# Five pads of 32 to 96 bytes that move activation tiles in SBUF, in a float32 two-block transformer on one core

## The chip, the cores and the metric

The kernel runs on one core of a Trainium2 chip (trn2). The metric is the device time of one execution in microseconds; the median of three runs of the kernel before is 1934.56 us (1934.15 to 1935.23). The other seven cores do nothing.

## The reference

One sequence of 256 tokens with 1024 features passes two blocks in float32. The first block is a mixer (retention in four heads, differential attention in four heads, both over the sequence and 256 context tokens) and a layer of 16384 single-neuron experts, of which eight retrieval heads choose 16 each per token. The second is a short convolution, attention to 256 memory tokens, a SwiGLU layer, causal attention in eight heads, memory attention and SwiGLU again. Cut to what carries the time:

```python
x = x + mod[:, 2] * (concat([ret_lat, diff_lat]) @ w_out)   # mixer
h2 = modulate(x, norm2_g, mod[:, 3], mod[:, 4])
u, vsel = expert_u[experts], expert_v[experts]              # 8 heads x 16 of 16384
act = gelu(einsum('thkd,td->thk', u, h2))
x = x + mod[:, 5] * einsum('thk,thkd->td', gate * act, vsel)
# second block: conv mixer, memory attention, SwiGLU, attention, memory attention, SwiGLU
```

## The kernel before

**Data.** Activations lie transposed in SBUF, 128 features on the partitions, eight chunks of features and 256 tokens on the free axis, so one chunk of one tile is 256 float32 values, 1024 bytes, on each partition. Weights stream through SBUF once, in tiles of 1024 values per partition (4096 bytes).

**The product.** A float32 product is three float32r passes. Each operand is split into a part that float32r holds (hi) and the rest (lo). `split_w` (L106 to L120) makes `whi` by a copy on ScalarE (L111) and `wlo` by a subtraction on VectorE or GpSimd (L115). `mm3` (L131) then issues, for eight chunks k, hi by hi, lo weight by hi and hi weight by lo, 24 matmuls into one PSUM bank (L137). Every matmul loads its own 128 by 128 stationary operand first (the rows on PEld). In `mm3` the weights are stationary and the activations are moved, 256 columns at a time:

```python
order = [(s, i) for s in range(3) for i in range(n)]
...
self.matmul = nc.tensor.matmul(out, a, b, start=..., stop=...)   # a stationary (weights), b moved
```

In `natural_steps` (L172) and in the expert product (L945) it is the other way round: the activations (`hh`, `hmh`, `acth`) are stationary and the weights are moved, 256 columns in the first, 512 in the second.

**The stages, in order of time.** Adaln parameters and the norm (to 92 us); mixer (to 306): gate, key, query and value products of `hh`, `hl`, attention, output product of `cath`, `catl` (L137), with tiles of the memory keys (`hmh`, `hml`) put in between; expert layer (306 to 1157): 16 query blocks and then 128 blocks of `peer_u`, 24 matmuls each, that move `h2h`, `h2l`. Beside them VectorE does the routing (top-k, L763 to L803), and after it, from `R1` = 16 pairs of blocks on, `group` (L867 to L885) builds the gates for four tokens at a time: GpSimd makes `ohA` (L861) and multiplies into `slots` (L882), VectorE and ScalarE make `ohB` (L862, L864), TensorE multiplies them (L876). 64 groups are spread over 96 blocks, so one group goes with 36 matmuls of `h2`. Then the expert product, 128 chunks of 12 matmuls (L945). The second block follows: convolution (1160 to 1277), memory attention, SwiGLU (`hh`, then `fh`, `fl`), attention (`hh`, `hqh`, `oh`), memory attention, SwiGLU, final norm.

**Where the tiles lie.** Pools are opened as a stack. A tile takes its size rounded up to 32 bytes, and a pool opens where the last open one ends. So a tile of 8 or 64 bytes early in a pool shifts all that opens later. The weight pool (`raw`, `whi`, `wlo`, L103, L109, L110) opens at byte 30432 and holds multiples of 4096: every weight tile starts at byte 224 of 512, which is byte 96 of 128. The starts of the others, counted in this way, on each partition, and those with the pads of the change counted in the same way:

| tiles | start before | of 512, before | of 512, with the pads |
|---|---|---|---|
| weights `whi`, `wlo` | 42720 and on | 224 | 224 |
| mixer `hh`, `hl` | 67296 | 224 | 256 |
| memory keys ahead, `hmh`, `hml` | 116480 | 256 | 288 |
| mixer `cath`, `catl` | 151936 | 384 | 416 |
| experts `slots`, `h2h`, `h2l`, `ohA`, `ohB`, `acth`, `actl` | 63200 and on | 224 | 256 |
| second memory, `memk1`, `memv1`, `hmh`, `hml` | 67296 | 224 | 256 |
| convolution `hh`, `hl`, `ch`, `cl` | 164704 | 352 | 0 |
| memory attention and SwiGLU `hh`, `fh`, `oh`; attention `hh` | 127744 and on | 256 | 384 |
| attention `hqh`, `hql`, `oh` | 164640 and on | 288 | 416 |

The chunks of these tiles and the columns of the weights go on in steps of 512 or 1024 bytes, so the place within 512 bytes holds for each matmul of a tile.

Of the kernel before, what the change touches and what calls it, by code (L numbers as in the profile page):

```python
"""A two-part transformer in one launch.

Activations lie transposed, features on the partitions and tokens on the free axis, and stay in
SBUF from the first norm to the last. Weights stream through SBUF once. A float32 product is
carried by three float32r passes: each operand is split into a part that float32r holds exactly
and the rest (hi + lo), and hi*hi + hi*lo + lo*hi are accumulated in PSUM.
"""
# [8 lines left out]
F32 = mybir.dt.float32  # L16
# [6 lines left out]
PSUM = bass.MemoryType.PSUM  # L23
DRAM = bass.MemoryType.DRAM

P = 128
T = 256
# [42 lines left out]
class Build:  # L70
# [14 lines left out]

    def banks(self, ctx, name):
        """The banks of one phase: mm and, by the phase, sc and aux or pairs of banks."""
        self.ps = ctx.enter_context(self.tc.tile_pool(name="psum" + name, bufs=2, space=PSUM))
# [5 lines left out]
    def after(self, ins, other):  # L94
        """Issue order only: no wait."""
# [22 lines left out]
    def weight(self, src, lo=None):  # L118
        """hi and lo of a weight tile. lo: the engine of the subtraction."""
# [7 lines left out]
    def mm3(self, out, pairs, first=True, last=True, late=False):  # L127
        """out += sum of w^T x over (w_hi, w_lo, x_hi, x_lo), three passes each; late: pair by pair."""
# [10 lines left out]
    def fill(self, n):  # L139
        """n tiles of the work that depends on nothing near."""  # L140
        for _ in range(n):
            next(self.filler, None)
# [6 lines left out]
    def block(self, out, src, x, cols=slice(None), lo=None, late=False, w=None):  # L149
        """out[128 n, tokens] = W block^T x, the weights stationary."""  # L150
# [8 lines left out]
    def natural_steps(self, tag, srcs, toks, done, lo=None):  # L159
        """x^T W with the tokens stationary, 256 columns of W (two tiles of srcs) at a time; two  # L160
        token blocks share a bank. done(n, i, bank) takes the columns n of the token blocks 2i, 2i + 1."""
# [26 lines left out]
    def rstd(self, pool, sums, n, tag, shape=(P, T), bufs=1, a=None, y=None, tables=False, behind=None):  # L188
        """(sums / n + eps) ** -0.5, a Newton step after the tables."""
# [19 lines left out]
    def track(self, x, m, tags=("acc", "accsq"), bufs=2):  # L209
        """Adds the squares of chunk m of eight to the sum over chunks; the last stays apart."""  # L210
# [10 lines left out]
    def tracked_norm(self, pool, tag, bank="aux", urgent=False, last=None, **kw):  # L221
        """rstd over the features of the chunks tracked, the same on every partition; last: behind the matmuls
        so far."""
# [17 lines left out]
    def modulated(self, pool, tags, x, r, A, Bv, h, cols):  # L241
        """h[:, :, cols] = x * r * A + B, split."""
# [8 lines left out]
    def gained(self, pool, x, gi, name="h"):  # L251
        """x * g (no rstd yet), split."""
# [46 lines left out]
    def mod_group(self, pool, g):  # L299
        """512 of the adaln parameters, for c and for c_ctx: the rows of o are hi c, hi c_ctx, lo c, lo c_ctx."""  # L300
# [31 lines left out]
    def mod_rest(self, pool, groups):  # L332
        """gate1, shift2, scale2, gate2 for c, a piece at a time."""
        nc, io = self.nc, self.io
        late = []
# [34 lines left out]
    def rope_out(self, pool, q, out, cos, sin):  # L370
        """out = q * cos + rot(q) * sin for q [128, 256] in SBUF; sin has the signs of rot, which swaps the halves
        of every 32 partitions."""
# [7 lines left out]
    def decay(self, pool, M):  # L380
        """M [j, t] for j in x and in ctx, by head: [128, 4 heads, 4 key chunks, 256]. The logarithms of the
        rates are not positive, so the smaller of the two exponents is the one for the sign of the distance."""
# [1235 lines left out]
```

## Time and profile before

| | |
|---|---|
| median of the runs (lowest, highest) | 1934.56 us (1934.15, 1935.23) |
| profiled execution, span | 1934.6 us |
| mean granted TensorE clock | 0.976 of full speed |
| HBM read | 329.59 MB, 172 GB/s over the span |

The profiled execution's own time is its span, from the first instruction to the last. A row of the timeline gives the start, the length from there, the engine, line and operation, the tiles as output <- moved operand, stationary operand, and the number of instructions merged. [...]

### The profile page before, as it was taken

What the parts mean: (1) busy time and instruction counts of PE and PEld (TensorE: products, weight loads), DVE (VectorE), ACT (ScalarE), POOL (GpSimd) and SP (SyncE); (2) the same over time, 40 slices, a digit from 0 to 9 for tenths busy, and PEclk for the clock granted to TensorE, in tenths of its full rate; (3) what the DMA queues carried; (4) which work ended last, traced back from release to release, by engine and by line L of the source; (5) the groups of instructions that cost most, each with busy time, mean ns of one, the idle gap of its engine ahead of it and who ended that gap; (6) DMA issues with size and microseconds to landing.
All of it is one profiled execution on the core that took longest, in us unless ns stands there. A gap on an engine that the chain in (4) does not pass through costs nothing.

```text
span 1934.6 us, 34858 instructions
## 1 busy us (share of the span) xinstructions
PE 1838.1 (95%) x13232; PEld 1717.9 (89%) x13232; DVE 1465.7 (76%) x2646; ACT 1043.2 (54%) x1775; POOL 587.3 (30%) x508
## 2 busy tenths in 40 slices
PE   5899999994999999999999998999999999999997
PEld 4697788994999999878888878999999998999997
DVE  8988966999988999865555568676765578677664
ACT  5645534542777777554554455455554544555543
POOL 2511113782888999400000004222000213110001
PEclk8999999997999999999999998999999999999999
DMA  7672434452444444655555555553555553435553
GB/s 261 218 250 93 137 131 154 170 179 76 167 161 164 164 153 160 225 195 194 196 195 191 192 184 177 185 185 132 195 187 187 187 179 130 158 127 186 187 191 124
DMA packets 99768, 335.15 MB, mean 173 GB/s; under 512 B 12400, under 2 KB 13456, under 8 KB 99216
## 3 DMA queue, kind: packets, MB, share of 16 engines
q1 hardware_dynamic: 98160, 330.68, 49.5%
q8 instruction: 105, 1.72, 0.4%
q10 hardware_dynamic: 1440, 2.23, 0.3%
q14 instruction: 63, 0.52, 0.1%
HBM read 329.59 MB, written 3.28 MB: 172 GB/s over the span
## 4 chain that ended last, share of the span: by engine, by line
PE 69%; DVE 16%; POOL 9%; DMA 2%; issue 2%; ACT 2%; SPq 0%; DVEq 0%; ACTq 0%; POOLq 0%
PE mm L137 40%; PE pair L945 17%; POOL ohA L861 5%; PE mm L172 4%; POOL slots L882 3%; PE fill L137 2%; DVE wlo L115 2%; PE fill L172 2%; DVE slots L798 1%; DVE slots L795 1%; PE pair L876 1%; PE sc L137 1%; DVE slots L773 1%; PE aux L137 1%; DVE mlo L115 1%
## 5 line engine op out<-in xcount | busy, mean ns | idle before, releaser
L111 ACT CAST whi<-raw 128x1024 fp32r<-128x1024 f32 x564 | 591.4, 1050 | 517.5 <-PE mm L137 261.0
L115 DVE TENSOR_TENSOR wlo<-raw,whi 128x1024 fp32r<-128x1024 f32 x490 | 623.9, 1276 | 297.7 <-PE pair L945 129.3
L115 POOL TENSOR_TENSOR wlo<-raw,whi 128x1024 fp32r<-128x1024 f32 x74 | 186.5, 2522 | 199.1 <-PE mm L137 109.0
L861 POOL TENSOR_SCALAR ohA<-iota,selT 128x128 fp32r<-128x128 f32 x256 | 191.1, 762 | 53.2 <-ACT selT L829 32.5
L219 POOL TENSOR_TENSOR acc<-acc,accsq 128x256 f32<-128x256 f32 x42 | 37.9, 903 | 497.9 <-ACT accsq L217 497.9
L137 PE MATMUL mm<-hh,whi 128*128 128x256 f32 (+1 forms) x1184 | 180.0, 289 | 6.2 <-DVE ct L1243 4.4
L137 PE MATMUL mm<-hl,whi 128*128 128x256 f32 (+1 forms) x1184 | 177.1, 287 | 1.0 <-DVE hl L262 0.9
L137 PE MATMUL mm<-hh,wlo 128*128 128x256 f32 (+1 forms) x1184 | 175.7, 286 | 0.6 <-DVE wlo L115 0.6
L137 PE MATMUL mm<-h2h,whi 128*128 128x256 f32 x1152 | 167.6, 288 | 4.1 <-ACT h2h L247 4.0
L137 PEld LDWEIGHTS mm<-hh,whi 128*128 128x128 f32 x1184 | 156.5, 190 | 11.1 <-issue 6.8
L137 PE MATMUL mm<-h2h,wlo 128*128 128x256 f32 x1152 | 163.4, 284 | 0.0
L137 PE MATMUL mm<-h2l,whi 128*128 128x256 f32 x1152 | 162.4, 284 | 0.0
L945 PE MATMUL pair<-whi,acth 128*128 128x512 f32 x512 | 158.4, 391 | 1.0 <-ACT acth L937 1.0
L137 PEld LDWEIGHTS mm<-hh,wlo 128*128 128x128 f32 x1184 | 155.0, 190 | 4.4 <-issue 1.5
L945 PE MATMUL pair<-whi,actl 128*128 128x512 f32 x512 | 158.2, 390 | 0.3 <-DVE actl L938 0.3
L137 PEld LDWEIGHTS mm<-hl,whi 128*128 128x128 f32 x1184 | 155.2, 190 | 3.4 <-DVE hl L262 1.6
L945 PE MATMUL pair<-wlo,acth 128*128 128x512 f32 x512 | 157.8, 389 | 0.0
L137 PEld LDWEIGHTS mm<-h2h,whi 128*128 128x128 f32 x1152 | 151.9, 195 | 5.0 <-ACT h2h L247 4.8
L137 PEld LDWEIGHTS mm<-h2h,wlo 128*128 128x128 f32 x1152 | 150.1, 193 | 0.0
L137 PEld LDWEIGHTS mm<-h2l,whi 128*128 128x128 f32 x1152 | 149.3, 193 | 0.0
L1083 POOL TENSOR_TENSOR memk0l<-kvt,memk0h 128x512 fp32r<-128x512 f32 x4 | 6.4, 1611 | 378.9 <-ACT memk0h L1082 378.9
L945 PEld LDWEIGHTS pair<-whi,acth 128*128 128x128 f32 x512 | 95.5, 188 | 22.1 <-ACT acth L937 2.6
(416 smaller groups left out, 3454.2 us busy)
## 6 DMA issues: line engine op xcount, KB each, us to landing
raw<-peer_u SPq DMA_DIRECT2D x128, 512.0 KB, 3.5
raw<-peer_v SPq DMA_DIRECT2D x128, 512.0 KB, 3.4
raw<-ffn_gu SPq DMA_DIRECT2D x88, 512.0 KB, 3.6
raw<-ffn_dn SPq DMA_DIRECT2D x44, 512.0 KB, 3.5
raw<-w_mod SPq DMA_DIRECT2D x64, 256.0 KB, 4.1
raw<-conv_wi SPq DMA_DIRECT2D x24, 512.0 KB, 3.5
raw<-mem_wk SPq DMA_DIRECT2D x16, 512.0 KB, 4.5
mraw<-w_mod SPq DMA_DIRECT2D x16, 512.0 KB, 6.4
```

The costliest lines, as they stand in the source:

```text
L111: self.hi_copy = nc.scalar.copy(hi, raw)
L115: (nc.vector if plan == "v" else nc.gpsimd).tensor_sub(lo, raw, hi)
L137: self.matmul = nc.tensor.matmul(out, a, b, start=first and j == 0, stop=last and j == 3 * n - 1)
L172: self.matmul = nc.tensor.matmul(outs[i // 2][:, i % 2], a[:, k, :], b[:, w], start=k == 0 and s == 0 and i % 2 == 0, stop=k == 7 and s == ...
L219: self.adder.tensor_add(self.acc, self.acc, self.last)
L773: nc.vector.tensor_tensor(cand, vv[:, :, 0, :, None].to_broadcast([P, 2, 16, 16]), vv[:, :, 1, None, :].to_broadcast([P, 2, 16, 16]), op=O ...
L795: nc.vector.tensor_tensor(one, pb[:, :, :, None].to_broadcast([P, 2, 16, 16]), self.iota[:, None, None, 0:16].to_broadcast([P, 2, 16, 16]) ...
L798: nc.vector.tensor_tensor(one, one, ii[:, :, side, None, :].to_broadcast([P, 2, 16, 16]), op=OP.mult)
L861: nc.gpsimd.tensor_scalar(A[:, i], self.iota, selT[:, 1, t:t + 1], None, op0=OP.is_equal)
L876: nc.tensor.matmul(o[:, 2 * j + i], A[:, i], Bt[:, i], start=True, stop=True)
L882: getattr(nc, GMUL).tensor_mul(sl, lo[:, :, :done], sl)
L945: nc.tensor.matmul(acc[th][:, dh], x[:, tsl], wt[:, dh * 512:dh * 512 + 512], start=c == 0 and s == 0, stop=c == NCH - 1 and s == 2)
```

## The change

A new helper puts a small tile into a pool, with a memset on VectorE that nothing reads. It is called in five places: first in the mixer's pool (32 bytes), first in the pool of `slots` (32), after `conv_w` in the convolution's pool (32), first in the pool `sums` of the second block (32) and first in the pool `side` (96 bytes). The weight pool opens ahead of all five. Comments are blanked besides.

```diff
+    def shift(self, pool, n=8):
+
+        self.nc.vector.memset(pool.tile([P, n], F32, name="shift"), 0.0)
+
...
             pool = self.pool(ctx, "mix")
+            self.shift(pool)
             rg = pool.tile([P, 4, T], F32, name="rg")
...
             big = self.pool(ctx, "slots")
+            self.shift(big)
             pool = self.pool(ctx, "peer")
...
             cw = self.load(pool, "conv_w", [P, KC, 3])
+            self.shift(pool)
             h = self.gained(pool, self.x, G_MIX)
...
                 b.sums = b.pool(c2, "sums")
+                b.shift(b.sums)
                 kvp = b.pool(c2, "kv")
                 side = b.pool(c2, "side")
+                b.shift(side, 24)
                 kv1, b.filler = b.mem_fill(kvp, side, 1)
```

## Rows read from the trace of the kernel before

**Rows 1.** The page, part 1: busy time of each engine, share of the span, instructions.

```profile
PE 1838.1 (95%) x13232; PEld 1717.9 (89%) x13232; DVE 1465.7 (76%) x2646; ACT 1043.2 (54%) x1775; POOL 587.3 (30%) x508
```

**Rows 2.** The page, part 4: the chain that ended last, by engine and line.

```profile
PE 69%; DVE 16%; POOL 9%; DMA 2%; issue 2%; ACT 2%; SPq 0%; DVEq 0%; ACTq 0%; POOLq 0%
PE mm L137 40%; PE pair L945 17%; POOL ohA L861 5%; PE mm L172 4%; POOL slots L882 3%; PE fill L137 2%; DVE wlo L115 2%; PE fill L172 2%; DVE slots L798 1%; DVE slots L795 1%; PE pair L876 1%; PE sc L137 1%; DVE slots L773 1%; PE aux L137 1%; DVE mlo L115 1%
```

**Rows 3.** Timeline of TensorE in the blocks of peer_u, h2 moved.

```profile
400.23 1.12 PE L137 MATMUL mm<-h2h,whi 128*128 128x256 f32 x8
...
403.11 1.12 PE L137 MATMUL mm<-h2h,whi 128*128 128x256 f32 x8
```

**Rows 4.** Timeline of TensorE in SwiGLU, fh moved, and in memory attention, oh moved.

```profile
1500.35 1.10 PE L137 MATMUL mm<-fh,whi 128*128 128x256 f32 x8
...
1505.95 1.10 PE L137 MATMUL mm<-fh,whi 128*128 128x256 f32 x8
...
1721.73 1.09 PE L137 MATMUL mm<-oh,wlo 128*128 128x256 f32 x8
...
1727.33 1.09 PE L137 MATMUL mm<-oh,wlo 128*128 128x256 f32 x8
```

**Rows 5.** Windows, TensorE alone: stretch, busy (matmuls), clock, DMA share, GB/s.

```profile
1740.00:1860.00 120.00, 120.00 (x1029) 1.00 0.53 185
```

**Rows 6.** Timeline of TensorE: the convolution's hh, and the second memory's hmh, moved.

```profile
1231.21 1.11 PE L137 MATMUL mm<-hh,whi 128*128 128x256 f32 x8
...
1236.90 1.12 PE L137 MATMUL mm<-hh,whi 128*128 128x256 f32 x8
...
1349.37 1.12 PE L137 MATMUL fill<-hmh,wlo 128*128 128x256 f32 x8
1350.33 1.12 PE L137 MATMUL fill<-hml,whi 128*128 128x256 f32 x8
```

**Rows 7.** Timeline of TensorE in the mixer's output product, cath moved.

```profile
283.38 1.10 PE L137 MATMUL mm<-cath,wlo 128*128 128x256 f32 x8
...
289.01 1.10 PE L137 MATMUL mm<-cath,wlo 128*128 128x256 f32 x8
```

**Rows 8.** Timeline of TensorE, weights moved, hh stationary: mixer, then second attention.

```profile
240.79 0.28 PE L172 MATMUL mm<-whi,hh 128*128 128x256 f32 x1
...
245.11 0.28 PE L172 MATMUL mm<-whi,hh 128*128 128x256 f32 x1
...
1552.78 0.28 PE L172 MATMUL mm<-whi,hh 128*128 128x256 f32 x1
...
1554.79 0.28 PE L172 MATMUL mm<-wlo,hh 128*128 128x256 f32 x1
```

**Rows 9.** Timeline of TensorE in the expert product, weights moved, 512 columns.

```profile
949.65 0.62 PE L945 MATMUL pair<-whi,actl 128*128 128x512 f32 x2
...
952.37 0.62 PE L945 MATMUL pair<-whi,actl 128*128 128x512 f32 x2
```

**Rows 10.** Windows of the experts: PE, PEld, DVE, ACT, POOL busy (count), clock, DMA, GB/s.

```profile
420.00:490.00 70.00, 43.54 (x344) 42.65 (x343) 69.15 (x237) 23.57 (x34) 32.38 (x18) 0.80 0.30 106
560.00:630.00 70.00, 70.00 (x586) 70.00 (x585) 63.38 (x122) 54.07 (x120) 61.34 (x75) 1.00 0.47 164
630.00:700.00 70.00, 70.00 (x585) 70.00 (x585) 68.59 (x121) 53.95 (x119) 68.84 (x74) 1.00 0.46 162
700.00:795.00 95.00, 90.65 (x716) 87.53 (x715) 91.31 (x150) 66.67 (x143) 94.75 (x91) 0.99 0.46 156
```

**Rows 11.** Lines L1245, L1290 (DVE), L1241, L376 (POOL): duration ns, minimum, median, maximum.

```profile
L1245 DVE TENSOR_TENSOR cl<-ct,ch x8: 410/419/426, 1199.3 to 1255.0; 128x256 fp32r<-128x256 f32 x8
L1290 DVE TENSOR_TENSOR fl<-fs,fh x44: 417/419/427, 1366.4 to 1864.2; 128x256 fp32r<-128x256 f32 x44
L1241 POOL TENSOR_TENSOR cy<-cy,nry x8: 728/738/895, 1195.8 to 1253.3; 128x256 f32<-128x256 f32 x8
L376 POOL TENSOR_TENSOR k<-qkt,pcos x8: 736/742/747, 1573.4 to 1595.1; 128x256 f32<-128x256 f32 x8
```

## The prediction, made before the change was run

> **What bounds the kernel now.** First the page: TensorE is busy 95% of the span [rows 1], and the chain that ended last is TensorE for 69%, VectorE for 16% and GpSimd for 9%; its largest pieces are the matmuls of L137 (40%) and of the expert product, L945 (17%) [rows 2]. So most of the time is a stream of matmuls without gaps, and the question is what one matmul costs in it. A merged row's own length does not tell that; the distance between starts does. Where `h2` is moved, 24 matmuls of 256 columns start within 403.11 - 400.23 = 2.88 us: 120.0 ns each [rows 3]. Where `fh` is moved, 48 of the same shape take 5.60 us, 116.7 each, and 48 of `oh` also 5.60, 116.7 [rows 4]. Windows that TensorE fills agree: 120.00 us hold 1029 matmuls of SwiGLU, 116.6 each [rows 5], and 70.00 us of `peer_u` hold 586, 119.5 each with the edges [rows 10]. [...]
>
> What separates the two is in the table of places. I call D the start of the moved operand less that of the stationary one, modulo 512 bytes. For `h2` both lie at 224, so D = 0; for `fh` and this `oh` it is 32. The other rows fit an order by D: the second memory's `hmh` with D = 0 takes 0.96 us per eight, 120.0 each, in the middle of the second block [rows 6], so it isn't the expert layer's traffic. The convolution's `hh`, at byte 96 of 128 like the weights but 128 bytes off (D = 128), takes 5.69 us for 48, 118.5 each [rows 6]. `cath` with D = 160 takes 5.63 us for 48, 117.3 [rows 7]. With the roles swapped, `hh` stationary at the weights' place (D = 0) costs 4.32 us for 36, 120.0; at 256 (D = 480) 2.01 us for 17, 118.2 [rows 8]. The expert product has D = 0 and takes 2.72 us for 12 matmuls of 512 columns, 226.7 each [rows 9]. I read this as a cost that both operands make together, highest where they have the same place within a block.
>
> [...]
>
> **The change, part by part.** Nothing of the work is removed; each stage gets another D. VectorE, ScalarE and GpSimd I cost at nothing: VectorE's subtraction takes 419 ns in the median with its tiles at byte 96 (L1245) and 419 at byte 0 (L1290), and GpSimd's product 738 at 96 (L1241) and 742 at 32 (L376) [rows 11].
>
> *Mixer, 92 to 306 us.* `hh` goes from D = 0 to 32. 240 matmuls of 256 columns gain 120.0 - 116.7 = 3.3 ns, 0.8 us; 384 with `hh` stationary go to D = 480 and gain 1.8, 0.7 us; 144 of 512 columns, taken at the same 1.8, 0.3 us. `cath` goes from 160 to 192 and the first `hmh` from 32 to 64, which I take as no change. Of these 1.8 us, about a third lies where attention on VectorE and ScalarE decides: 1.2 us.
>
> *Expert layer, 306 to 795 us.* All 3456 matmuls of `h2` go from D = 0 to 32, which would be 3456 x 3.3 = 11.4 us if TensorE decided throughout. It doesn't. From 420 to 490 VectorE is busy 69.15 of 70 us and TensorE 43.54 [rows 10]: the routing ends this part, TensorE waits for it after its 16 pairs of blocks, and faster matmuls before only lengthen the wait. I take 0.3 us there, since the queries that start the routing come sooner. From 484 on TensorE decides: a group with its blocks takes 40 x 0.120 = 4.8 us, and GpSimd is busy 61.34 of 70. But GpSimd's part of a group grows, and from about 639 it is full: 68.84 of 70, then 94.75 of 95, while TensorE falls to 90.65 [rows 10]. There TensorE would only wait for `ohA`. So the gain counts for (639 - 484) / 4.8 = 32 groups of 36 matmuls: 1152 x 3.3 = 3.8 us. With a pace that is 2.5% shorter GpSimd fills up some four groups sooner, which takes back 4 x 36 x 3.3 = 0.5. Together 0.3 + 3.8 - 0.5 = 3.6 us; bounds 1 (GpSimd full from the start of the groups on) and 11.4.
>
> *Expert product, 803 to 1157 us.* TensorE decides alone. The weights stay at 224 and the stationary `acth`, `actl` go to 256: D = 480. No row has 512 columns there. The nearest is the pair of `hh` rows with the roles swapped in the same way, 1.8 ns per matmul [rows 8]: 1536 x 1.8 = 2.8 us. Bounds: nothing, if 512 columns hide it, and the 3.3 ns of D = 32, 5.1 us.
>
> [...] No row here comes below 226 with 512 columns.
>
> *Convolution, 1160 to 1290 us.* D goes from 128 to 288, which has no row; 288 is 32 past a multiple of 128, as 160 and 32 are, and I take the 117.3 of 160: 768 x 1.2 = 0.9 us. The second memory's `hmh`, which fills in here and later, goes from 0 to 32: 192 x 3.3 = 0.6, and 192 with it stationary x 1.8 = 0.3. Together 1.8 us; bounds 0.6 and 2.6.
>
> *The rest, 1290 to 1925 us: a loss.* The 32 bytes of `sums` and the 96 of `side` move everything behind by 128. `hh`, `fh` and `oh`, well placed before (D = 32), go to D = 160: 2688 + 1056 + 384 = 4128 matmuls from 116.7 to the 117.3 of `cath`, 0.6 each: 2.5 us lost, TensorE being the bound there. Bounds 0 and 7.4 (118.5, the row of D = 128). `hqh` and the last `oh` go from 64 to 192: 384 matmuls, taken as nothing, 0.2 either way.
>
> *The memsets.* Five on VectorE, not shown in the trace. They stand at the start of a pool, behind the VectorE work that used the place last, and nobody reads them; what is queued behind each is the first chunk of the next stage. I take 0.1 us in all, bounded by 0 and by five subtractions of 0.42, 2.1 us. No DMA is added or moved.
>
> Sum: -1.2 - 3.6 - 2.8 - 1.8 + 2.5 + 0.1 = -6.8 us against the span of 1934.6, which is the median of the runs (1934.56) too: 1927.8 us.
>
> **The rivals.** 1: *more of it.* The other stages take the full 3.3 ns and the part behind 1290 us loses nothing, as `oh` and `fh` agree while `cath` is only one small stage: -1.2 - 3.6 - 5.1 - 2.6 = -12.5, 1922.1 us. 2: *place is not the cause*, and the rows differ by what runs beside them: 1934.6. Against it: `hmh` at 120.0 stands between rows of 116.7 in the second block. 3: *gains and losses cancel.* D = 160 costs as much as D = 128 over 4128 matmuls (+7.4) and 512 columns hide theirs: -1.2 - 3.6 - 1.8 + 7.4 = +0.8, 1935.4. 4: *slower.* The 4128 matmuls behind 1290 us fall to the full 120.0, since a shift by 128 bytes meets the weights again: +13.6 - 9.4 = +4.2, 1938.8. It decides from a loss of 2.3 ns per matmul (9.4 us / 4128) on, 119.0 ns; against it stands `cath`, which has this D and takes 117.3.
>
> **How the numbers follow.** The forecast gets 0.60, rivals 1 to 4 get 0.17, 0.08, 0.09 and 0.06. Changes below 0.2%, 3.9 us, a measurement of this kernel can't tell from none. Between 1930.7 and 1938.4 lie rivals 2 and 3 and, of the forecast, some 0.10, where GpSimd fills up early or the expert product gains nothing. Faster 0.67, same 0.27, slower 0.06. The range goes from 1917, where rival 1 meets a GpSimd part that speeds up in step, to 1935, which takes in rivals 2 and, nearly, 3.
>
> **What the changed profile would show.** Eight matmuls of `h2` in 0.93 to 0.94 us instead of 0.96; the expert product's pairs 0.450 apart instead of 0.453; `fh` at 0.94 instead of 0.93 per eight; TensorE waiting longer for the routing near 470 us, and GpSimd full from some point before 639 on. I am wrong in the mechanism if `h2` still starts every 120 ns, and wrong in the sum if GpSimd's stretch from 639 to 795 changes length, which no row here excludes.

## The result and the profile after

The changed kernel takes 1948.18 us (median of 4 runs, 1945.74 to 1949.26) against 1934.36 for the kernel before beside it (4 runs, 1934.00 to 1935.23): ratio 1.007, 95% interval 1.0056 to 1.0084. It is **slower by 13.8 us**; the forecast was 6.8 us faster, in a range from 1917 to 1935. The runs' times lie some 1.8 us above the spans, which the traces are told in from here. So the profiled execution of the kernel before, with its span of 1934.6, was by estimate a run of 1936.4, some 2 us above the median of its runs, and the differences between traces come out that much smaller than those between medians. The profiled execution has a span of 1945.8 us at a mean granted clock of 0.974. A second profiled execution of the same kernel, called *again* below, was taken later (1948.92 us, span 1947.1).

Parts 1 and 4 of the page of the changed kernel, to be set beside [rows 1, 2]:

```profile
PE 1838.5 (94%) x13232; PEld 1708.9 (88%) x13232; DVE 1471.2 (76%) x2651; ACT 1042.9 (54%) x1775; POOL 589.4 (30%) x508
PE 70%; DVE 17%; POOL 8%; issue 2%; ACT 2%; DMA 1%; DVEq 0%; SPq 0%; ACTq 0%; POOLq 0%
```

No share moved by more than a point, and the only new work is VectorE's five memsets (2651 instructions for 2646). What grew has to be looked for by stage. The table gives each stage's length, from the starts of its first instructions in the traces; differences named in the text are taken before rounding:

| stage, from the first to the first of the next | before | after | again | forecast of the difference |
|---|---|---|---|---|
| to the first `hh` matmul of the gates | 92.0 | 97.3 | 92.5 | 0 |
| mixer, to the first `h2h` | 214.6 | 211.9 | 213.8 | -1.2 |
| routing, to its last transpose | 176.6 | 179.2 | 179.7 | -0.3 |
| groups, to the first matmul of the expert product | 319.4 | 315.6 | 316.2 | -3.3 |
| expert product, to its last matmul | 354.2 | 362.2 | 363.1 | -2.8 |
| convolution, to the first memory scores | 137.8 | 136.9 | 136.1 | -1.8 |
| the rest | 640.0 | 642.7 | 645.8 | +2.5 |

The first stage varies from trace to trace: over the kernels told of here it lies anywhere from 90.1 to 97.3 us, with and without pads. The mixer behind it is mostly shorter where the first stage is longer (209.8 after 95.4 in second_only, which has no pad in the mixer), so its row says little by itself. The timeline of TensorE in the changed kernel shows the others: `h2` moved, the expert product, `fh` in the first SwiGLU, `hh` in the second.

```profile
400.46 1.09 PE L141 MATMUL mm<-h2h,whi 128*128 128x256 f32 x8
...
403.26 1.09 PE L141 MATMUL mm<-h2h,whi 128*128 128x256 f32 x8
...
1000.26 0.63 PE L951 MATMUL pair<-whi,acth 128*128 128x512 f32 x2
...
1003.06 0.63 PE L951 MATMUL pair<-whi,acth 128*128 128x512 f32 x2
...
1509.95 1.10 PE L141 MATMUL mm<-fh,whi 128*128 128x256 f32 x8
...
1512.76 1.10 PE L141 MATMUL mm<-fh,whi 128*128 128x256 f32 x8
...
1839.77 1.12 PE L141 MATMUL mm<-hh,whi 128*128 128x256 f32 x8
...
1842.62 1.11 PE L141 MATMUL mm<-hh,whi 128*128 128x256 f32 x8
```

Here `h2` takes 2.80 us for 24 matmuls, 116.7 ns each, where it took 120.0 [rows 3]. The expert product takes 2.80 us for 12, **233.3 ns** where it took 226.7 [rows 9]. The two SwiGLU layers, with the same place D = 160, differ: 2.81 us for 24 in the first, 117.1 each, and 2.85 in the second, 118.8 (116.7 before, rows 4).

Windows of the expert layer in the changed kernel, columns as in [rows 10]:

```profile
420.00:490.00 70.00, 37.08 (x303) 36.29 (x303) 69.76 (x241) 20.89 (x28) 29.88 (x12) 0.76 0.27 91
630.00:700.00 70.00, 69.71 (x589) 69.01 (x588) 69.03 (x121) 52.74 (x116) 68.30 (x74) 1.00 0.50 165
700.00:795.00 95.00, 88.94 (x719) 85.28 (x718) 92.25 (x151) 68.11 (x146) 95.00 (x91) 1.00 0.48 155
```

As forecast, TensorE waits longer for the routing (37.08 of 70 us busy, 43.54 before), and GpSimd is full at the end (95.00 of 95).

The routing itself, which I had costed as unchanged work on VectorE, became 2.7 us longer (3.1 in again), and VectorE's busy time in it grew by 3.1 us. One line grew from 1.5 to 8.1 us, as three of its eight conversions met GpSimd; other instructions of VectorE gave a part of it back, most of all L779 (L773 before), with 11.0 us instead of 13.7. First the line's durations (minimum, median, maximum in ns), before and after, then the collision in the timeline of the changed kernel, GpSimd's row and VectorE's:

```profile
L769 DVE CAST slots<-slots x8: 177/182/186, 334.2 to 472.7; 128x64 f32<-128x64 uint32 x8
```

```profile
L775 DVE CAST slots<-slots x8: 180/186/2393, 336.1 to 477.9; 128x64 f32<-128x64 uint32 x8
402.72 2.45 POOL L119 TENSOR_TENSOR wlo<-raw,whi 128x1024 fp32r<-128x1024 f32 x1 [0.35 <-PE mm L141]
402.84 2.39 DVE L775 CAST slots<-slots 128x64 f32<-128x64 uint32 x1
```

A conversion of 64 columns, 0.18 us before, took 2.39 us in three places of the changed kernel's trace, at 377.60, 402.84 and 428.05 us. GpSimd's subtraction had begun 0.08 to 0.13 us ahead of it each time, and the two ended within 0.1 us of each other (here at 405.23 and 405.17 us). What inside the chip holds the conversion up, no trace shows.

### The profile page after: what moved, and what is told of

The parts are those of the page before. It is cut to its first block, busy times and chain, and to the rows that moved or that the text cites. A ratio compares the mean times of both kernels' runs of the same rounds, so it can differ in the third digit from the quotient of the medians.

```text
span 1945.8 us, 34864 instructions
## 1 busy us (share of the span) xinstructions
PE 1838.5 (94%) x13232; PEld 1708.9 (88%) x13232; DVE 1471.2 (76%) x2651; ACT 1042.9 (54%) x1775; POOL 589.4 (30%) x508
## 4 chain that ended last, share of the span: by engine, by line
PE 70%; DVE 17%; POOL 8%; issue 2%; ACT 2%; DMA 1%; DVEq 0%; SPq 0%; ACTq 0%; POOLq 0%
PE mm L141 40%; PE pair L951 18%; POOL ohA L867 5%; PE mm L176 4%; POOL slots L888 3%; PE fill L176 2%; DVE slots L804 1%; PE fill L141 1%; DVE wlo L119 1%; PE sc L141 1%; DVE slots L801 1%; PE pair L882 1%; DVE mlo L119 1%; PE aux L141 1%; DVE slots L779 1%
## 5 line engine op out<-in xcount | busy, mean ns | idle before, releaser
L141 PE MATMUL mm<-hl,whi 128*128 128x256 f32 (+1 forms) x1184 | 176.6, 287 | 0.8 <-DVE hl L266 0.8
L141 PE MATMUL mm<-h2h,wlo 128*128 128x256 f32 x1152 | 159.3, 280 | 0.0
L141 PE MATMUL mm<-h2l,whi 128*128 128x256 f32 x1152 | 158.5, 280 | 0.0
L141 PEld LDWEIGHTS mm<-h2h,wlo 128*128 128x128 f32 x1152 | 146.2, 189 | 0.0
L141 PEld LDWEIGHTS mm<-h2l,whi 128*128 128x128 f32 x1152 | 145.3, 189 | 0.0
L951 PEld LDWEIGHTS pair<-whi,actl 128*128 128x128 f32 x512 | 96.1, 188 | 24.4 <-DVE actl L944 1.4
```

What stands on the lines that cost most here:

```text
L141: self.matmul = nc.tensor.matmul(out, a, b, start=first and j == 0, stop=last and j == 3 * n - 1)
L951: nc.tensor.matmul(acc[th][:, dh], x[:, tsl], wt[:, dh * 512:dh * 512 + 512], start=c == 0 and s == 0, stop=c == NCH - 1 and s == 2)
```

## Experiments

Hypothesis after the result: the place sets what a matmul costs, but the order of the places is another one for 512 columns, and D = 160 is worse than `cath` said. Rivals: traffic beside the matmuls, or pads that did something else. The first four runs: the costs by themselves, and the change in three parts.

**probe.** The model is left out and the input returned; TensorE runs streams of 96 matmuls of 256 columns (48 of 512) with nothing beside them, each with another D. In `stream`, behind the name and the width, stand the starts of the moved and the stationary operand, in values of 4 bytes, and the number of matmuls: `p` and `q` move D on by 32 bytes at a time, the four `t` streams hold D at 192 and move both operands on.

```diff
+        for j in range(16):
+            stream("p" + names[j], 256, 8 * j, 0, 96)
+        for j in range(16):
+            stream("q" + names[j], 512, 8 * j, 0, 48)
...
+        for j in range(4):
+            stream("t" + names[j], 256, 8 * j + 48, 8 * j, 96)
```

> This kernel leaves the whole model out and returns its input; it only issues streams of matmuls with nothing beside them, stationary and moved operand at 16 distances D (start of the moved operand less start of the stationary one, modulo 512 bytes, in steps of 32), 96 of 256 columns and 48 of 512 columns at each, and four pairs of streams in which both operands are moved together. Theory A (the place of the two operands to each other alone sets the cost, and with 512 columns the order is reversed): 256 columns cost 120.0 ns at D = 0, 116 to 118 at 32, 114 to 116 at 192; 512 columns cost 226.7 at D = 0 and 233 at 32 and 480; moving both operands together changes less than 1 ns. Rival B (traffic of the other engines makes the difference): all sixteen streams of a width cost the same within 1 ns, since nothing runs beside them.

Rows of its timeline, one stream each (`pa` D = 0, `pf` 160, `pg` 192, `ph` 224, `qa` 0, `qb` 32):

```profile
23.58 11.68 PE L1487 MATMUL pa<-mv,wt 128*128 128x256 f32 x96
35.10 11.47 PE L1487 MATMUL pb<-mv,wt 128*128 128x256 f32 x96
...
80.62 11.43 PE L1487 MATMUL pf<-mv,wt 128*128 128x256 f32 x96
91.89 11.07 PE L1487 MATMUL pg<-mv,wt 128*128 128x256 f32 x96
102.80 11.52 PE L1487 MATMUL ph<-mv,wt 128*128 128x256 f32 x96
...
204.72 11.09 PE L1487 MATMUL qa<-mv,wt 128*128 128x512 f32 x48
215.65 11.37 PE L1487 MATMUL qb<-mv,wt 128*128 128x512 f32 x48
226.85 11.16 PE L1487 MATMUL qc<-mv,wt 128*128 128x512 f32 x48
```

From `pa` to `pb` 11.52 us, 120.0 ns each; from `qb` to `qc` 11.20, 233.3. Mean distances between starts in the last two thirds of each stream, at a granted clock of 1.00; from D = 256 on the same values come again, so the period is 256 bytes, not the 512 I had taken:

```
D             0      32     64     96     128    160    192    224
256 columns   120.0  117.8  117.8  120.0  118.7  117.4  113.3  118.3
512 columns   226.7  233.3  228.9  233.5  233.4  234.2  233.4  233.4
```

Traffic isn't needed for any of it. D = 0 is the worst place for 256 columns and **the best for 512**. With both operands moved on together, D = 0 kept its 120.0 in four streams more. One thing didn't fit: at D = 192 the four `t` streams took 113.3, 117.8, 113.3, 117.8.

**The parts alone:** `mix_only` has the mixer's pad, `experts_only` that in the pool of `slots`, `second_only` the three of the second block.

> The kernel before with the pad of the mixer's pool alone. Theory A (matmul spacings by D): 256 columns of hh gain 3 ns x 240 = 0.7 us, hh stationary 1.6 x 384 = 0.6, 512 columns lose 4 x 144 = 0.6, cath gains 2 x 192 = 0.4: 0 to 1 us faster, 1933.5 to 1934.5. Rival C (the first 306 us are later by how VectorE and GpSimd meet there): 2 to 3 us slower, 1936.5 to 1937.5, the first matmul of the gates at 97 us instead of 92.

> The kernel before with the pad of the pool of slots alone. Theory A: the groups gain 3.6 us up to 639 us and nothing after, and the expert product loses 1536 x 6.4 = 9.8 us: 5 to 7 us slower, 1939.5 to 1941.5. Rival D (the expert product is slow only together with the shifts of the other stages, or the trace's stage was one slow execution): within 2 us of the kernel before or faster by the groups' 3.6 us, 1930.5 to 1936.5. If the routing is longer too, as in the changed kernel (2.7 us), up to 1944.

> The kernel before with the three pads of the second block alone. Theory A: D = 160 instead of 32 costs 1.2 ns x 4128 = 5.0 us behind 1290 us, D = 192 for hqh and the last oh gives back 2.5 ns x 384 = 1.0, the convolution and the second memory's tiles 1.0: 2.5 to 4 us slower, 1937 to 1938.5. Rival E (the second block carries none of it): within 1 us of the kernel before.

| run | median us (runs) | ratio to before, 95% interval |
|---|---|---|
| mix_only | 1933.79 (12) | 1.0001 (0.9991 to 1.0011) |
| experts_only | 1942.42 (5) | 1.0046 (1.0033 to 1.0060) |
| second_only | 1937.98 (12) | 1.0022 (1.0013 to 1.0031) |

The three add up to 1.0069, the change has 1.0070. Two thirds of the loss come from the expert layer's 32 bytes. In `second_only` the first SwiGLU, same D = 160, has yet another price; its timeline:

```profile
1511.14 1.12 PE L140 MATMUL mm<-fh,whi 128*128 128x256 f32 x8
...
1514.02 0.88 PE L140 MATMUL mm<-fh,whi 128*128 128x256 f32 x6
```

2.88 us for 24: 120.0 ns, the price that rival 4 had named; its second SwiGLU has 117.5.

**Undoing one half, and the best places by the probe.** `acts_back` keeps the change and puts `acth` back to D = 0. `h2_alone` is the kernel before with only `h2` moved. `rest_back` puts the second block back to D = 32. `best` moves every moved activation tile to D = 192 (mod 256).

The second argument of `shift` counts values of 4 bytes, 8 where it isn't given; the edits in short:

```text
acts_back:  the change, and self.shift(pool, 120) first in the experts' pool
h2_alone:   self.shift(big) and self.shift(pool, 120) as there, no other pad
rest_back:  the change with b.shift(side, 120) instead of b.shift(side, 24)
best:       mix 48, before cath 24, slots 48, experts 16, sums 48, side 56, conv 40, before kT 56
```

> The change, and a pad of 480 bytes first in the experts' pool, so that acth and actl lie again where they lay before against the weights (D = 0); all else as in the change. Theory A (a matmul of 512 columns costs 226.7 ns at D = 0 and 233.4 at any other place): the distance between the starts of the pairs' matmuls goes back from 233 to 226.7 ns, the stage of L945 from 362 to about 354 us, and the whole by 8 to 10 us, to 1938 to 1940 us. Rival B (that stage became longer for what VectorE, ScalarE and the DMAs do beside it, not for the place of acth): within 3 us of the change, 1945 to 1949 us, and 233 ns stay.

> The kernel before with two pads only: 32 bytes first in the pool of slots, 480 bytes first in the experts' pool; so h2 goes to D = 32 and the expert product stays at D = 0. Theory A (the routing gives back what the faster h2 gains, because VectorE meets GpSimd's subtractions, now 2.80 instead of 2.88 us apart, at other instructions): the matmuls of h2 take 116.7 ns, the 64 groups gain 3 to 4 us until 639 us, the turn that ends the routing comes 2 to 4 us later than 483.2, the casts of the indices take 8 instead of 1.5 us, and the whole is within 2 us of 1934, not told from no change. Rival B (the late routing in the runs so far had to do with the other pads): the routing ends no later than before, and the whole comes to 1929.5 to 1931.5 us.

> The change with 480 bytes instead of 96 in the pool side, so that the tiles of the second block behind 1290 us lie as before against the weights (hh, fh, oh at D = 32, hqh at 64), and the convolution at D = 160. Theory A (D = 160 costs 118.0 and D = 32 costs 116.8 ns in these 4128 matmuls; hqh and the last oh lose what D = 192 gave): hh, fh and oh back at 116.7 to 116.9 ns, 5 us gained there, 2 to 3 lost again with hqh, oh and the convolution: 2 to 4 us below the change, 1943.5 to 1946 us. Rival B (the place within 512 bytes does not set these matmuls, a shift by 128 is no loss): the same as the change within 1 us and 118.0 ns stay.

> Pads of 64 to 224 bytes instead of those of the change (192 first in the mixer's pool, 96 ahead of cath, 192 in the pool of slots, 64 in the experts' pool, 192 in sums, 224 in side, 160 in the convolution's pool, 224 ahead of the attention's kT): every moved activation tile goes to D = 192 (of 256), the expert product stays at D = 0. Theory A (the order of the stream probe holds in the kernel): all moved products at 113.3 to 113.9 ns, expert product at 226.7; behind 1290 us 4512 matmuls gain 3 ns or more each, 13 us; convolution 4, attention and mixer 2 to 3; the expert layer 0 to 6, since GpSimd ends its groups: 1907 to 1917 us. Rival B (in the kernel the weights are written and read beside the matmuls and hide what the probe showed): h2, fh and hh stay at 116 to 118 ns and the whole within 5 us of 1934.

| run | median us (runs) | ratio, 95% interval | what its trace shows |
|---|---|---|---|
| acts_back | 1937.18 (12) | 1.0023 (1.0009 to 1.0036) | expert product 354.7 us, 226.7 ns |
| h2_alone | 1932.54 (12) | 0.9991 (0.9981 to 1.0002) | `h2` 117.1 ns, routing 179.2 us |
| rest_back | 1942.90 (6) | 1.0047 (1.0031 to 1.0062) | `hh`, `fh` 116.7 ns, the rest 637.9 us |
| best | 1931.99 (12) | 0.9999 (0.9986 to 1.0012) | convolution, `oh` 113.3 to 113.6; `h2` 117.3, SwiGLU 117.8 ns |

Timeline of TensorE in acts_back's expert product:

```profile
1000.22 0.62 PE L951 MATMUL pair<-whi,actl 128*128 128x512 f32 x2
...
1002.94 0.62 PE L951 MATMUL pair<-whi,actl 128*128 128x512 f32 x2
```

2.72 us for 12 again. With the place of `acth` alone undone, 11.0 of the change's 13.8 us are gone by the medians (1948.18 - 1937.18), 9.1 by the ratios, since the two were measured at different times, and 7.4 or 8.4 by the stage's length in the traces. The distances say 1536 x 6.7 = 10.2; the stage's gaps, what distances over 0.3 us have beyond the steady one, vary beside that from 4.0 to 7.6 us in sum over all traces. In h2_alone the faster `h2` is there and the whole can't be told from no change: the routing, 2.6 us longer, takes a good half of the 4.3 us that the groups gain. Over all traces told of here with the routing's code unchanged, it is 178.9 us or longer in eleven of the twelve with moved `h2` (once 176.9, in best3), and 176.6 to 176.8 in the three with `h2` at its old place. The same pad moves the routing's own tiles, so no run separates their place from that of `h2`; best3, with best2's pads and 2.0 us less, shows that the place alone doesn't set the length. Undoing the second block's shift is worth 5.3 us by the medians (4.4 by the ratios), more than the 2 to 4 expected. And `best` was a miss: tiles of equal D took 113.3 in one stage and 117.8 in another, and both at one place: the memory attention's `oh` and SwiGLU's `fh` have D = 448 of 512 alike.

**probe2: is it chance at a break?** In `best` the distance changed in mid-stage, from 113.4 to 117.8 ns at a short accumulation of the norm's sums, and stayed. I call such a distance that a stream keeps its rhythm, and a wait or a short accumulation between streams a break. Rival: copies and transfers beside the matmuls. The model is left out again; each of 96 streams stands behind a short matmul, half of these behind a wait for VectorE.

```diff
+        def stop(name, j):
+            if j >= 8:
+                nc.vector.tensor_copy(tmp[:, :8 * (j - 7)], out[0][:, :8 * (j - 7)])
+            n = 8 * (j - 7) if j >= 8 else 8 + 6 * j
...
+            nc.tensor.matmul(o[:, :n], wt[:, :P], tmp[:, :n], start=True, stop=True)
```

> Leaves the model out and returns its input: 96 streams, each behind a short matmul of another width, half of these behind a wait for VectorE. 80 streams of 96 matmuls of 256 columns, 16 at each of D = 0, 32, 160, 192, 448; 16 of 48 matmuls of 512 columns, 8 at D = 0, 8 at D = 224. Theory A (the place allows a few rhythms, and the break ahead of a stream picks one, which lasts until the next break): streams of one D fall into two or three sharp groups, 113.3 and 117.8 ns at D = 192 and 448, 116.7 and 117.8 at D = 32, 117.3, 118.7 and 120.0 at D = 160, while D = 0 has 120.0 alone, and 512 columns 226.7 at D = 0 and 233 to 234 at D = 224 whatever the break. Rival B (the place alone decides, and in the kernel it is the copies and transfers beside the matmuls that raise 113.3 to 117.8): all 16 streams of one D agree within 0.3 ns, 113.3 at D = 192 and 448. About 1000 us.

Timeline: two streams at D = 192 (`hj`, `hk`) and two at 448 (`ij`, `ik`), the same program but for the width of VectorE's copy and of the short matmul ahead:

```profile
572.95 11.14 PE L1508 MATMUL hj<-mv,wt 128*128 128x256 f32 x96
584.36 0.28 PE L1500 MATMUL bij<-tmp,wt 128*128 128x16 f32 x1 [0.27 <-DVE tmp L1497]
584.49 11.55 PE L1508 MATMUL ij<-mv,wt 128*128 128x256 f32 x96
...
632.38 11.55 PE L1508 MATMUL hk<-mv,wt 128*128 128x256 f32 x96
644.21 0.28 PE L1500 MATMUL bik<-tmp,wt 128*128 128x24 f32 x1 [0.27 <-DVE tmp L1497]
644.34 11.15 PE L1508 MATMUL ik<-mv,wt 128*128 128x256 f32 x96
```

The lengths, 11.14 and 11.55 us, change places. What stands ahead includes the stream before: in all 16 pairs the stream at 448, which comes next after that at 192 behind a short matmul, has the other of the two distances. Mean distances in the last two thirds of the 16 streams of a D (8 with 512 columns), counted:

```
D = 0     120.0 x16
D = 32    116.7 x14   117.8 x2
D = 160   117.3 to 117.4 x13   118.6 x2   120.0 x1
D = 192   113.3 x14   117.8 x2
D = 448   113.3 x2    117.8 x14
512 columns: D = 0 226.7 x8; D = 224 233.3 to 233.4 x8
```

Theory A holds in each item: in probe2 a place has one to three sharp rhythms, what stands ahead of a stream picks one, and it lasts. With 512 columns each of the two places has one. What in the wait or the short matmul decides isn't shown.

**best2 and again.** `best2` moves what lay at 448 in `best` to 192; `again` is the changed kernel a second time.

```text
b.shift(side, 120) instead of b.shift(side, 56); 64 more in the convolution and before kT, to hold their place
```

> The kernel best with 256 bytes more in the pool side (480 instead of 224), and the pads of the convolution and of kT 256 larger too: the tiles of the second block that lay at D = 448 (hh, fh, oh) go to D = 192, the rest stays. Theory A (D = 192 and D = 448 have the same two rhythms, but the same break picks the other one, so what ran at 117.8 ns runs at 113.3): SwiGLU and the projections of hh behind 1290 us at 113.3 to 114 ns, 4128 matmuls x 4 = 16 us off, 1914 to 1920 us. Rival B (which rhythm comes up is decided by what ends last ahead of each stage, not by the 256 bytes): one SwiGLU or none at 113.3, the whole at 1922 to 1933 us.

> The changed kernel once more, unaltered, for one profiled execution. If the rhythm of a stage follows from the program alone, the two SwiGLU layers show 117.3 and 118.7 ns again, within 0.2; if chance at a break decides, at least one of them shows another of 117.3, 118.7 and 120.0 ns. The expert product shows 233 to 235 ns in either case. 1945 to 1951 us.

best2: 1929.85 us (12 runs, **1919.72 to 1940.98**), ratio 0.9983 (0.9965 to 1.0001); its profiled execution has both SwiGLU layers at 117.8, so nearer rival B: 256 bytes don't decide. It was one of the slower executions (1935.09), and no fast one was profiled. again: both SwiGLU layers at 118.6 to 118.8 ns where the first had 117.3 before, so the program alone doesn't pick; 1.4 ns on the first layer's 1584 matmuls are 2.2 of the 3.1 us by which its rest is longer.

**probe3: can a break be steered?** 70 pairs of streams at D = 192, ten each with nothing, with 1, 2 or 3 matmuls of 8 columns, or with one of 32, 64 or 128 columns between the two of a pair (the model left out).

> Leaves the model out and returns its input: 70 pairs of streams at one place (stationary at 224, moved at 416, D = 192, as SwiGLU in best2), 48 matmuls of 256 columns each; a wait for VectorE ahead of every first stream, and between the first and the second nothing, or 1, 2 or 3 matmuls of 8 columns, or one of 32, 64 or 128. Theory A (the wait picks the rhythm by chance, and a short matmul in between can turn 117.8 into 113.3): the first streams fall into 113.3 and 117.8 ns; with nothing between, the second goes on in the rhythm of the first; with one kind of short matmul at least 8 of 10 second streams are at 113.3 whatever the first was. Rival B (a short matmul turns each rhythm into the other, or leaves it): no kind brings more than 7 of 10 to 113.3 other than from what the first was. About 900 us.

Timeline, a pair with two short ones between, and a pair with one:

```profile
132.00 5.70 PE L1511 MATMUL ccb<-mv,wt 128*128 128x256 f32 x48
137.53 0.28 PE L1499 MATMUL scb<-mv,wt 128*128 128x8 f32 x2
137.67 5.69 PE L1511 MATMUL dcb<-mv,wt 128*128 128x256 f32 x48
...
203.89 5.70 PE L1511 MATMUL cbc<-mv,wt 128*128 128x256 f32 x48
209.43 0.17 PE L1499 MATMUL sbc<-mv,wt 128*128 128x8 f32 x1
209.45 5.90 PE L1511 MATMUL dbc<-mv,wt 128*128 128x256 f32 x48
```

5.70 and 5.69 are the 113.3 rhythm, 5.90 is 117.8. With nothing between, all 10 second streams go on as the first. One or three short matmuls turn 113.3 into 117.8 in 24 of 24 cases, and 117.8 into 113.3 in 16 of 26; two leave 113.3 alone in 5 of 5 and turn 117.8 into 113.3 in 2 of 5. No kind brings 8 of 10 to 113.3 whatever came before, so that part of theory A fell; but two at a time lost nothing in these ten and sometimes gained.

**best3, after_pairs, best4.** Two short matmuls ahead of every third accumulation: in best2's second block, in the change's, and in best2's first block too.

```diff
+        if first and n > 2 and getattr(self, "short", False):
+            self.count = getattr(self, "count", 0) + 1
+            if self.count % 3 == 0:
+                for _ in range(2):
+                    nc.tensor.matmul(out[:, :8], pairs[0][0], pairs[0][2][:, :8], start=True, stop=True)
```

> best2, and in the second block two matmuls of 8 columns ahead of every third accumulation of TensorE (they write into the bank that the accumulation then starts anew). Theory A (a wait picks the rhythm by chance, two short matmuls keep 113.3 ns and turn 117.8 into 113.3 in a part of the cases, so a stage falls into 113.3 and stays): both SwiGLU layers run at 113.3 to 114.5 ns for most of their length, behind 1290 us 14 to 18 us less than with 117.8, the spread of the runs shrinks, median 1915 to 1921 us. Rival B (in the kernel something beside the matmuls, copies or transfers, holds them at 117.8): SwiGLU stays at 117.8, the short matmuls cost 1 to 3 us, median 1930 to 1934 us, and the spread stays.

> The change, and the same two short matmuls ahead of every third accumulation in the second block, D = 160 there as in the change. Theory A (at D = 160 too a rhythm is picked at a break, and the low one, 117.3 ns, is kept): both SwiGLU layers at 117.3 to 117.6 ns, where the change had 117.3 or 118.7 in one and 118.7 in the other; 2 to 5 us below the change, 1943 to 1946.5 us. Rival B (at D = 160 the rhythm follows from what ends ahead of the stage, and the short ones change nothing or lead to 120.0): 118.7 or 120.0 ns, 1948 to 1955 us.

> best3 with the two short matmuls in the first block too, ahead of every third accumulation (mixer and the blocks of peer_u; not in the expert product). Theory A: h2, at D = 192, falls to 113.3 to 114.5 ns; until 639 us that gives the groups 1 to 3 us, then GpSimd decides; with best3's gain 1912 to 1920 us, at most 3 us below best3. Rival B (GpSimd ends the expert layer whatever TensorE does, and the short matmuls cost their 0.03 us each): the same as best3 within 2 us or up to 2 us slower.

best3: 1933.30 us (11 runs, 1927.07 to 1935.47), ratio 0.9994 (0.9986 to 1.0003), with both SwiGLU layers at **113.3 to 113.4 ns**, the first from end to end, the second but for its first blocks: the mechanism as expected, the price not. The profiled execution was the fastest of the eleven, so for the median this isn't shown. Its timeline:

```profile
1386.54 1.07 PE L145 MATMUL mm<-hl,whi 128*128 128x256 f32 x8
1387.45 0.28 PE L141 MATMUL mm<-hh,whi 128*128 128x8 f32 x2
1387.59 1.16 PE L145 MATMUL mm<-hh,whi 128*128 128x256 f32 x8
1388.58 1.07 PE L145 MATMUL mm<-hh,wlo 128*128 128x256 f32 x8
```

From 1387.45 to 1388.58 are 1.13 us where eight matmuls alone take 0.906: 0.22 us for a pair, not the 0.03 to 0.06 I had taken from probe2, where I had left out that the second long matmul starts 200 ns after the first. At that price the 65 pairs of its second block (47 of them ahead of `hh`) cost some 14.6 us, an estimate, and ate the gain. after_pairs: 1956.00 (4 runs), ratio 1.0104 (1.0089 to 1.0119), 7.8 above the change: the same price, and at D = 160 the pairs found no lower rhythm for good (120.0, 118.6 and 117.4 ns follow each other in its SwiGLU layers); rival B. best4: 1934.07 (12 runs), ratio 0.9993 (0.9983 to 1.0004), 0.8 above best3: in its trace `h2` has 115.4 ns between full matmuls where best3 has 115.7, so the pairs hardly moved it and 59 more of them had to be paid for. The time is rival B's; whether GpSimd would have hidden a faster `h2` isn't shown.

**best5: a few pairs at the start of each layer.** best2 with a pair ahead of the gate block of chunks 2 to 7 and of outputs 1 and 2 of each SwiGLU layer, 16 in all.

```diff
+                    self.short = i == 0 and 1 < m < 8
...
+                    self.short = n == 0 and m in (1, 2)
```

> best2 with the two short matmuls at few places: ahead of the gate block of the chunks 2 to 7 of each SwiGLU layer and of its outputs 1 and 2, 16 in all instead of one at every third accumulation. Theory A (113.3 ns stays once it is there, so a few tries at the start of a layer do): both SwiGLU layers at 113.3 ns from the first third on; against best2's profiled execution with 117.8 in both, 14 us less for 3168 matmuls and 16 x 0.23 = 3.6 us more for the short ones: median 1920 to 1926 us, below the kernel before. Rival B (the low rhythm is lost again within a layer, and it took the frequent short ones to hold it): parts of the layers back at 117.8, median 1928 to 1934 us.

1924.34 us (5 runs, 1921.80 to 1926.90) against 1932.30: ratio **0.9950** (0.9936 to 0.9964), below both kernels, and with best2's pads alone the ratio was 0.9983 (0.9965 to 1.0001). The start of its first SwiGLU in the timeline:

```profile
1365.98 1.11 PE L144 MATMUL mm<-hh,wlo 128*128 128x256 f32 x8
1366.92 1.10 PE L144 MATMUL mm<-hl,whi 128*128 128x256 f32 x8
1367.86 0.28 PE L140 MATMUL mm<-hh,whi 128*128 128x8 f32 x2
1368.00 1.17 PE L144 MATMUL mm<-hh,whi 128*128 128x256 f32 x8
1369.01 1.07 PE L144 MATMUL mm<-hh,wlo 128*128 128x256 f32 x8
1369.92 1.07 PE L144 MATMUL mm<-hl,whi 128*128 128x256 f32 x8
1370.83 1.07 PE L144 MATMUL mm<-hh,whi 128*128 128x256 f32 x8
```

Eight matmuls take 0.94 us ahead of the pair and 0.91 behind it, and so it stays to the layer's end, in the second layer too, in the slowest of the five executions. What lies behind the convolution takes 631.2 us, 640.0 in the kernel before; theory A.

**cast_act and best6: the routing.** The conversion that meets GpSimd is given to ScalarE, in h2_alone and in best5.

```diff
-nc.vector.tensor_copy(z["i"], z["iu"])
+nc.scalar.copy(z["i"], z["iu"])
```

> h2_alone with the conversion of the indices of the routing (8 times 64 columns) on ScalarE instead of VectorE. From the first h2 matmul to the last transpose of the routing the kernel before takes 176.5 us and h2_alone 179.2. Theory A (the routing became longer because this conversion now meets GpSimd's subtraction and stands 2.4 us in its way, three times): 175 to 177 us. Rival B (VectorE only meets GpSimd at the next instruction instead, the sum stays): 178 to 180 us. The whole 1929 to 1934 us.

> best5 with that conversion on ScalarE. Theory A: the routing 2 to 4 us shorter than best5's 179.1, and as the groups after it are ended by GpSimd from about 639 us on, the whole 2 to 4 us shorter: 1920 to 1923 us. Rival B: the collision moves on to the next instruction: 1923 to 1926 us, the same as best5.

A miss by both: cast_act 1947.09 us (one run), best6 1935.68 (12 runs, ratio 1.0005, 0.9996 to 1.0015). The routing takes 194.3 us in cast_act and 192.9 in best6. Groups of VectorE in the routing (306 to 500 us), first of cast_act, then of h2_alone: busy us, mean ns.

```profile
L807 DVE COPY slots<-slots 128x32 f32<-128x32 f32 x8 | 11.2, 1402 | 0.0
L791 DVE TENSOR_SCALAR slots<-slots 128x32 uint32<-128x32 uint32 x8 | 9.4, 1178 | 0.0
```

```profile
L807 DVE COPY slots<-slots 128x32 f32<-128x32 f32 x8 | 7.4, 920 | 0.0
L791 DVE TENSOR_SCALAR slots<-slots 128x32 uint32<-128x32 uint32 x8 | 3.3, 411 | 0.0
```

The collisions move on to other short instructions, as rival B had it, but their sum does not stay: the instructions of 512 columns lose more than these gain (L802 has 26.8 us in h2_alone and 17.0 in cast_act), and VectorE's busy time in the routing falls from 169.4 to 164.6 us. The 15 us more have another cause. ScalarE, whose queue also makes `whi`, sits idle for VectorE ahead of the conversions, 60.8 us in all, and at the end VectorE waits for ScalarE's exponentials (L816). First the answer on the conversions, then the line behind the exponentials, both of cast_act:

```profile
L773 ACT CAST slots<-slots x8: 244/244/245, 332.1 to 460.4; 128x64 f32<-128x64 uint32 x8
...
  DVE slots L771: 60.8, 8
```

```profile
L822 DVE TENSOR_REDUCE slots<-slots 128x8 f32<-128x128 f32 x2 | 0.5, 284 | 18.9 <-ACT slots L816 18.9
```

Up to the exponentials VectorE was done 163.7 us after the first `h2` matmul, 9.4 us sooner than in h2_alone (best6: 10.0 sooner than best5), and then stood idle for 18.9 us. So VectorE's part was shorter with the conversion on ScalarE, and the wait for ScalarE ate the gain. What the collision costs the routing by itself stays open all the same: with `whi` later, GpSimd's subtractions came later too, so other meetings changed with it.

## Why the prediction was wrong

**The step that failed** is the expert product's: "The nearest is the pair of `hh` rows with the roles swapped in the same way, 1.8 ns per matmul [rows 8]: 1536 x 1.8 = 2.8 us. Bounds: nothing, if 512 columns hide it, and the 3.3 ns of D = 32, 5.1 us." Both bounds were gains; no reason excluded a loss. It rested on the reading that the cost is "highest where they have the same place within a block". That order does not carry over from 256 columns to 512: D = 0 is the best there. 1536 matmuls went from 226.7 to 233.3, which is 10.2 us lost where 2.8 were to be won; the stage became 8.0 and 8.9 us longer in the two traces, mostly because its gaps were 1.8 and 1.0 us shorter in sum, and undoing the place gave 9 to 11 us. Of the 20.6 us between forecast and measurement some 11 are this step. The trace of before had no row of 512 columns at another D, which was a reason to bound the term from both sides and to let a rival stand on it.

Point by point:
- *The place sets the cost of a matmul:* right, shown by the probe without other work and by acts_back. Rival 2 (no change, as the place is not the cause) is excluded: with nothing beside the matmuls, places that lie multiples of 32 bytes apart differ by up to 6.7 ns in the probe (120.0 at D = 0, 113.3 at 192). No stream of 512 columns here came below 226.7 ns.
- *`h2` from 120.0 to 116.7, groups 3.3 us, GpSimd full at the end:* right (3.8 and 3.1 us in the two traces, 3.2 to 4.6 in the others with `h2` at D = 32; 116.7 ns). That it fills up sooner than at 639 doesn't show: 68.30 of the 70 us from 630 on, 68.84 before.
- *Routing 0.3 us shorter:* wrong, 2.7 and 3.1 longer. GpSimd follows TensorE (it stands idle for it 0.40 us ahead of the subtraction at 371.92 us, and 0.47 ahead of that at 370.86 before), so its subtractions come every 2.80 us instead of 2.88, and VectorE meets them at other instructions. That the meeting is the cause is read from the trace; the run that was to show it did not.
- *Convolution -1.8:* -0.9 and -1.7, with 117.8 and 116.7 ns, two rhythms of the same place (D = 288, which is 32 of 256). *Mixer -1.2:* -2.7 and -0.9, but mix_only can't be told from no change; its 144 matmuls of 512 columns lost (227.9 to 233.2 ns) instead of gaining.
- *The rest +2.5, from `cath`'s 117.3:* +2.7 and +5.8, with 4.4 to 5.3 by the runs of rest_back. The value was one of three that this place has. Rival 4's 120.0 came up in second_only, as one rhythm of the place, not as what the shift always does. Two terms were left out or put at nothing: the second attention's 192 matmuls with `hh` stationary went from 118.2 to 120.0 ns, and the attention's `oh`, at D = 192, went from 117.8 to 113.4 in one of the two traces.
- *The memsets, 0.1 us:* 0.07 to 0.08 us each, five of them; what they delay is not shown.
- *Rivals:* only the third (+0.8) and the fourth (+4.2) lay above the kernel before, with 0.15 together, and neither had a loss in the expert product. The fourth got 0.06, and its sign came true for another reason.

The sum again with measured terms (table above, mean of the two traces without the first stage): -1.8 + 2.9 - 3.5 + 8.5 - 1.3 + 4.2 = +9.0. The first stage has +2.8 in these traces, and 11.8 is the difference of the spans; the other 2 us of the 13.8 are, by estimate, the profiled execution of the kernel before, which the prediction took for its median run.

## What to carry over

A price read at one shape did not bound the price at another (D = 0 had the highest with 256 columns, 120.0 ns, and the lowest with 512, 226.7): put a loss into the range of a term that has no row of its own shape. Where an inner loop is a stream of matmuls, measure the stream alone, with each place of the operands and more than once, before moving tiles; one row of a place may be one of several rhythms (117.3, 118.6 and 120.0 ns at D = 160). A gain on TensorE, which GpSimd follows, changed when GpSimd met VectorE (every 2.80 us instead of 2.88), and the unchanged routing beside it became 2.7 and 3.1 us longer: look at every stage beside a gain.

## What the runs showed of the hardware

- For float32r, one weight load per matmul, the distance between starts depends on the places of the two operands to each other, with a period of 256 bytes in the probe: 113.3 to 120.0 ns for 256 columns, 226.7 to 234.2 for 512, and in opposite order at D = 0. What inside the chip does it was not looked into.
- At 256 columns a place has up to three rhythms (113.3 or 117.8; 116.7 or 117.8; 117.3, 118.6 or 120.0). In probe3, at D = 192, all 10 second streams with nothing between went on as the first; one or three short matmuls turned 113.3 into 117.8 in 24 of 24 cases, two in none of 5. The choice of rhythm may also make a part of the spread of the runs, an estimate from best2's 12, which span 21 us, and best6's 12, where pairs set it, 6.
- A pair of 8-column matmuls in such a stream cost 0.22 us in best3, as much as two full ones at 113.3 ns.
- A conversion of 64 columns on VectorE took 2.39 us instead of 0.18 where it started 0.08 to 0.13 us behind GpSimd's subtraction, and ended within 0.1 us of it (three times in the changed kernel).
